# A decoder trunk in float32 by split products: some low parts made by an accumulating transfer, and the order of TensorE fixed in four places

## The chip, the cores and the metric

The kernel runs on one core of one Trainium2 chip. The time is device microseconds of that core for one execution of the program, lower is better. The engines are named as in the profile: PE is TensorE (matmuls), PEld its weight loads, DVE is VectorE, ACT is ScalarE, POOL is GpSimd, SP is SyncE (here it only issues transfers).

## The reference

Two layers over x of shape (1, 512, 1024) in float32, with D_FF = 1408:

```python
def swiglu_ffn(h, w_gu, w_down):
    a, b = jnp.split(h @ w_gu, 2, axis=-1)
    return (jax.nn.silu(a) * b) @ w_down

for i in range(DEPTH):                         # DEPTH = 2
    x = x + 0.5 * swiglu_ffn(rms_norm(x, ffn1_norm[i]), ffn1_w_gu[i], ffn1_w_down[i])
    h = rms_norm(x, mix_norm[i])
    x = x + (mla_gla_mixer(h, ...) if i % 2 == 0 else stick_breaking_mixer(h, ...))
    x = x + 0.5 * swiglu_ffn(rms_norm(x, ffn2_norm[i]), ffn2_w_gu[i], ffn2_w_down[i])
    gate = jax.nn.sigmoid(rms_norm(x, ple_norm[i]) @ ple_w_gate[i])
    x = x + gate * (p[i] @ ple_w_proj[i])
return rms_norm(x, final_norm)
```

Each mixer ends in a product with an output matrix (`ev_w_out`, `od_w_qkv`'s partner `od_w_out`); `ple_w_gate` is the gate of the per-layer embedding.

## The kernel before

x stands transposed in eight tiles of 128 x 512 (features by tokens). Every float32 product is three fp32r products (`mm3`, L393 to L395): both operands are split into a high part, which is a rounding copy, and a low part, which is the rest, and high by high, low by high and high by low are summed. For a weight this is `w_cut` (L260, L261): ACT casts the loaded tile `wr` into `wh`, and DVE subtracts, `wl = wr - wh`. A tile is 128 x 1024 (or 768). Eight matmul steps of three are 24 matmuls on one such weight.

Weights go through three stages, in the order of a list `plan` of all of them: SP loads `wr` from memory (L256, at most 8 tiles), `w_split` cuts it at most WS = 4 weights ahead of the product that uses it, and PE uses it. The kinds that matter here are `gu` (first feed-forward's gate and up weights, pairs A and B, ten tiles, of which the first two are cut in quarters at the start), `sg` (units of the other gate and up columns), `pg` (gate of the embedding, eight tiles, layer 0), `oo` (output matrix of layer 1's mixer, eight tiles, of which the first OPEN = 3 are held in other buffers) and `dn`.

`start` and `gates` compute the first 640 columns of layer 0's first feed-forward. `gated` (L790 to L794) then applies the gate to each pair. All other gate and up columns go through `ffn7`, which computes a 2 x 2 block product with seven products instead of eight: B11, B21, T1, T2, B22, T3, T4, in this order in the program. Each uses two units of weights; T1 to T4 need differences of the loaded tiles, which DVE makes in place (`w_term`, L289), before the cut. The other operands are tiles of the normed x: `nvh`, `nvl` for B11 (even tiles of x), `noh`, `nol` for B21 (odd tiles), `nuh`, `nul` for T1 and T2 (both). `Norm7.steps` (L529 to L569) makes them on ACT and DVE as each tile of x gets its last addition, and adds up squares in `sqa` (L489). One product on one group of columns is 2 tiles x 4 steps x 3 matmuls (L704 to L706). After T1, `norm.sums()` sums `sqa` over features with eight small matmuls into `pss` (L587); DVE (L600) and POOL (L602) make the factor `rc` of them, which `close` uses later. B21's result is added by DVE at L724, and copies of the accumulators are made by ACT (L719).

The text of the kernel is not the order that the engines run. The framework's list scheduler places the instructions by its own estimates; where an instruction is made with `tc.keep_in_program_order`, it keeps its place among the others so made. In the kernel before, a small class `Queue` does this for DVE in `ple` only (profile rows of that stretch carry line 123), and `w_pin` for the cuts of T1's weights in the first group of columns. PE's order is the scheduler's.

## Time and profile before

| what | value |
|---|---|
| median of 3 runs | 1315.92 us (1312.94 to 1319.41) |
| profiled execution, its own time | 1318.16 us |
| its span in the trace | 1316.4 us |
| mean granted clock of PE | 0.983 |
| PE busy | 1280.7 us, 97% |
| DVE busy | 910.8 us, 69% |
| ACT busy | 665.1 us, 51% |
| POOL busy | 116.9 us, 9% |
| read from memory | 115.50 MB |

The profiled execution is 2.24 us above the median; 1.8 us of its time lie outside its span. A busy PE is one with a matmul in flight: one on 512 columns follows the last after about 0.23 us at full clock, and one on 384 columns after about 0.17 us.

### The profile page before, as it was taken

The numbers are of one execution on the slowest core, as the hardware profiler recorded it, in microseconds if no ns is written. First come the engines' busy times: TensorE is split into PE (matmuls) and PEld (weight loads), VectorE is DVE, ScalarE is ACT, GpSimd is POOL, SyncE is SP. The second block draws the span as 40 slices with busy tenths as digits, with TensorE's granted clock in tenths as the row PEclk, the third lists the DMA queues.
The fourth block names the chain that finished last, engine by engine and source line by source line (L and its number), as shares of the span: only waits on it lengthen the run. The fifth ranks groups of instructions, "written<-read, shape, count | busy, mean of one in ns | idle before, by whom it ended". The sixth has DMA issues, their size and how long they took to land.

```text
span 1316.4 us, 16266 instructions
## 1 busy us (share of the span) xinstructions
PE 1280.7 (97%) x6212; PEld 1092.2 (83%) x6212; DVE 910.8 (69%) x1316; ACT 665.1 (51%) x1064; POOL 116.9 (9%) x132
## 2 busy tenths in 40 slices
PE   9969999998999999999989999999999999999997
PEld 7869888886888888988868898888888887898886
DVE  6688763579775998654799875445767598885544
ACT  6455352432654565542655553334778556554442
POOL 0001000425350000000000000000111000000000
PEclk9979999999899999999989999999999999999999
DMA  7023343111300032533203343322113003224401
GB/s 290 34 88 117 109 147 106 45 64 41 121 17 17 0 128 97 160 128 111 81 1 128 97 129 111 128 97 96 65 59 102 16 16 128 93 85 142 145 1 64
DMA packets 39454, 118.66 MB, mean 90 GB/s; under 512 B 4615, under 2 KB 5768, under 8 KB 39376
## 3 DMA queue, kind: packets, MB, share of 16 engines
q1 hardware_dynamic: 38016, 114.64, 26.2%
q0 software_dynamic: 640, 1.89, 0.5%
q8 instruction: 49, 0.80, 0.2%
q10 hardware_dynamic: 720, 1.09, 0.2%
q14 instruction: 29, 0.24, 0.1%
HBM read 115.50 MB, written 2.10 MB: 89 GB/s over the span
## 4 chain that ended last, share of the span: by engine, by line
PE 87%; DVE 9%; ACT 2%; issue 1%; SPq 0%; DMA 0%; POOL 0%; POOLq 0%; DVEq 0%; ACTq 0%
PE dn L395 6%; PE dn L394 6%; PE dn L393 6%; PE al L704 5%; PE al L705 5%; PE al L706 5%; PE ga L705 3%; PE ga L704 3%; PE ga L706 3%; PE sqk L393 2%; PE sqk L395 2%; PE sqk L394 2%; PE val L1016 2%; PE val L1018 2%; PE val L1017 2%; DVE wl L261 1%
## 5 line engine op out<-in xcount | busy, mean ns | idle before, releaser
L260 ACT CAST wh<-wr 128x1024 fp32r<-128x1024 f32 (+3 forms) x299 | 275.4, 925 | 362.2 <-PE dn L394 81.5
L261 DVE TENSOR_TENSOR wl<-wr,wh 128x1024 fp32r<-128x1024 f32 (+3 forms) x292 | 312.7, 1075 | 168.1 <-ACT wh L260 167.4
L395 PE MATMUL dn<-gh,wl 128*128 128x512 f32 x352 | 137.4, 390 | 0.3 <-DVE wl L261 0.2
L393 PE MATMUL dn<-gh,wh 128*128 128x512 f32 x352 | 137.0, 392 | 0.7 <-ACT wh L260 0.7
L394 PE MATMUL dn<-gl,wh 128*128 128x512 f32 x352 | 137.2, 390 | 0.0
L289 DVE TENSOR_TENSOR wr<-wr,wr 128x1024 f32<-128x1024 f32 (+1 forms) x88 | 94.9, 1097 | 0.2
L395 PEld LDWEIGHTS dn<-gh,wl 128*128 128x128 f32 x352 | 66.1, 188 | 14.9 <-DVE wl L261 1.2
L393 PEld LDWEIGHTS dn<-gh,wh 128*128 128x128 f32 x352 | 66.0, 188 | 14.5 <-ACT wh L260 1.1
L394 PEld LDWEIGHTS dn<-gl,wh 128*128 128x128 f32 x352 | 66.1, 188 | 13.8 <-DVE gl L401 0.6
L602 POOL TENSOR_TENSOR rc<-v,half 128x4 f32<-128x4 f32 x8 | 11.8, 1480 | 683.5 <-DVE v L600 683.5
L704 PE MATMUL al<-wh,nvh 128*128 128x512 f32 (+1 forms) x176 | 64.6, 367 | 4.7 <-ACT nvh L534 4.7
L705 PE MATMUL al<-wl,nvh 128*128 128x512 f32 (+1 forms) x176 | 64.5, 366 | 0.0
L706 PE MATMUL al<-wh,nvl 128*128 128x512 f32 (+1 forms) x176 | 64.3, 367 | 0.0
L637 DVE SCALAR_TENSOR_TENSOR x<-dn,x 128x512 f32<-128x512 f32 x32 | 22.1, 691 | 40.9 <-PE dn L395 40.9
L393 PE MATMUL sqk<-xnh,wh 128*128 128x512 f32 x128 | 50.2, 393 | 0.0
L395 PE MATMUL sqk<-xnh,wl 128*128 128x512 f32 x128 | 50.0, 390 | 0.0
L394 PE MATMUL sqk<-xnl,wh 128*128 128x512 f32 x128 | 49.9, 390 | 0.0
L704 PE MATMUL ga<-wh,nuh 128*128 128x512 f32 (+1 forms) x88 | 34.6, 406 | 6.3 <-ACT wh L260 6.3
L704 PEld LDWEIGHTS al<-wh,nvh 128*128 128x128 f32 x176 | 33.2, 189 | 8.9 <-ACT nvh L534 5.1
L481 ACT ACTIVATE sq<-x 128x512 f32<-128x512 f32 x64 | 39.2, 622 | 0.0
L1016 PE MATMUL val<-wh,xnh 128*128 128x512 f32 x96 | 37.5, 391 | 0.0
L1018 PE MATMUL val<-wh,xnl 128*128 128x512 f32 x96 | 37.4, 389 | 0.0
(462 smaller groups left out, 3293.6 us busy)
## 6 DMA issues: line engine op xcount, KB each, us to landing
wr<-in_sg SPq DMA_DIRECT2D x48, 512.0 KB, 4.0
wr<-in_sg SPq DMA_DIRECT2D x40, 384.0 KB, 3.3
wr<-in_dn SPq DMA_DIRECT2D x32, 384.0 KB, 3.1
wr<-in_dn SPq DMA_DIRECT2D x32, 320.0 KB, 3.5
wr<-in_od_qk SPq DMA_DIRECT2D x16, 512.0 KB, 3.2
wr<-in_ev_in SPq DMA_DIRECT2D x12, 512.0 KB, 3.5
wr<-in_gu SPq DMA_DIRECT2D x8, 512.0 KB, 7.2
wr<-in_ev_out SPq DMA_DIRECT2D x8, 512.0 KB, 3.2
```

What stands on the lines that cost most here:

```text
L260: pin(act.copy(hi[:, cs], t[:, cs]))
L261: pin(dve.tensor_tensor(lo[:, cs], t[:, cs], f32(hi)[:, cs], op=ALU.subtract))
L289: sub = lambda o, x, y: pin(dve.tensor_tensor(o[:, :n], x[:, :n], y[:, :n], op=ALU.subtract))
L393: pe.matmul(acc, wh, xh, start=start, stop=False, **k)
L394: pe.matmul(acc, wh, xl, start=False, stop=False, **k)
L395: pe.matmul(acc, wl, xh, start=False, stop=stop, **k)
L481: ins = act.activation(sq, x[m], AF.Square)
L704: pe.matmul(o, h[:, cs], wh[:, ws], start=begin, stop=False, skip_group_check=True)
L705: pe.matmul(o, h[:, cs], wl[:, ws], start=False, stop=False, skip_group_check=True)
L706: pe.matmul(o, lw[:, cs], wh[:, ws], start=False, stop=end, skip_group_check=True)
L1016: pe.matmul(accs[b], xn[k][0][:, bs], wh[:, ws], start=k == 0, stop=False)
L1018: pe.matmul(accs[b], xn[k][1][:, bs], wh[:, ws], start=False, stop=k == KD - 1)
```

## The change

Two things.

First, for three kinds of weight (`gu` from the third tile on, `pg`, and the five `oo` tiles that are not held) the low part is made another way. ACT casts `wh` as before, then ACT writes `wl = -wh`, and POOL issues a transfer that adds the weight from memory to `wl` (512 KB, the same bytes that SP has loaded). 8 + 8 + 5 = 21 subtractions of DVE become 21 ACT instructions and 21 transfers. The others, `sg` and `dn` among them, stay.

Second, PE gets the same `Queue`, and for the first group of columns of each of the four `ffn7` its matmuls of B11, B21, T1 and T2 keep the order of the program. `norm.sums()` moves behind T2. (In layer 0's first feed-forward `rc` is there already, so there it is not called.)

```diff
+        def __init__(self, engine):
+            self.engine, self.kept = engine, False
         def __getattr__(self, name):
-            call = getattr(nc.vector, name)
+            call = getattr(self.engine, name)
...
-    dve = Queue()
+    dve, pe = Queue(nc.vector), Queue(nc.tensor)
...
+    def w_cut_dma(t, src, n, hi, lo):
+        act.copy(hi[:, :n], t[:, :n])
+        act.activation(lo[:, :n], f32(hi)[:, :n], AF.Copy, scale=-1.0)
+        pool.dma_start(lo[:, :n], src, accum_op=ALU.add)
...
             ready[i] = parts
+        elif plan[i][0] in BY_DMA and needs[i] > FIRST:
+            ready[i] = w_tiles()
+            w_cut_dma(t, loads[needs[i] - 1][0], n, *ready[i])
         else:
...
         for gi, (_, n) in enumerate(groups):
             two = lambda name: [bank(name) for _ in range(2)]
+            pe.kept = gi == 0
             al = two("al")
             product(al, gi, "B11", True, False)
...
             product(ga, gi, "T1", True, False)
+            c22 = copies(ga, n)
+            product(al, gi, "T2", False, False)
             if rc is None:
                 rc = norm.sums()
-            c22 = copies(ga, n)
-            product(al, gi, "T2", False, False)
+            pe.kept = False
             c12 = copies(al, n)
...
+BY_DMA = ("pg", "oo", "gu")
```

Three places show what this does to the order of instructions.

ACT at the start of the program, where the casts of the third to the sixth `gu` tile stand (`wr` is the loaded tile, `wh` its high part, `sq` a square for the norm). Before:

```order
L260 CAST wh_236<-wr_226 128x1024
L260 CAST wh_242<-wr_228 128x1024
L260 CAST wh_248<-wr_230 128x1024
L260 CAST wh_260<-wr_232 128x1024
L481 ACTIVATE sq_266<-x_72 128x512
```
With the change:

```order
L280 CAST wh_236<-wr_226 128x1024
L281 ACTIVATE wl_237<-wh_236 128x1024
L280 CAST wh_243<-wr_228 128x1024
L281 ACTIVATE wl_244<-wh_243 128x1024
L280 CAST wh_250<-wr_230 128x1024
L280 CAST wh_263<-wr_232 128x1024
L281 ACTIVATE wl_251<-wh_250 128x1024
L281 ACTIVATE wl_264<-wh_263 128x1024
```
The negations stand between the casts and in front of the squares. On PE, the first products with these weights (A and B are the accumulators, `xnh` and `xnl` the parts of x) are now in this order, and the first with a low part comes after the high ones of three tiles; before it came third:

```order
L404 MATMUL A_300<-xnh_127,wh_236 128x512
L405 MATMUL A_300<-xnl_129,wh_236 128x512
L404 MATMUL B_332<-xnh_127,wh_243 128x512
L405 MATMUL B_332<-xnl_129,wh_243 128x512
L404 MATMUL A_364<-xnh_127,wh_250 128x512
L405 MATMUL A_364<-xnl_129,wh_250 128x512
L406 MATMUL A_300<-xnh_127,wl_237 128x512
L404 MATMUL A_300<-xnh_141,wh_236 128x512
L405 MATMUL A_300<-xnl_143,wh_236 128x512
```
DVE in the first feed-forward, first group (`nul`, `nwl`, `nvl`, `nu` are operands of the norm's steps; `wr<-wr,wr` a difference of weights). Before:

```order
L560 SCALAR_TENSOR_TENSOR nw_546<-x_75,gains,nu_567 128x256
L567 TENSOR_TENSOR nul_574<-nu_567,nuh_571 128x512
L261 TENSOR_TENSOR wl_694<-wr_254,wh_693 128x768
L569 TENSOR_TENSOR nwl_548<-nw_546,nwh_547 128x256
L532 TENSOR_TENSOR nv_577<-nv_577,ne_578 128x256
L289 TENSOR_TENSOR wr_256<-wr_356,wr_256 128x768
L538 TENSOR_TENSOR nvl_584<-nv_577,nvh_582 128x512
L558 SCALAR_TENSOR_TENSOR nu_586<-x_77,gains,ne_578 128x256
L289 TENSOR_TENSOR wr_254<-wr_396,wr_254 128x768
L559 TENSOR_TENSOR nu_586<-nu_586,nv_577 128x256
L289 TENSOR_TENSOR wr_356<-wr_470,wr_356 128x768
```
With the change:

```order
L571 SCALAR_TENSOR_TENSOR nw_554<-x_75,gains,nu_575 128x256
L578 TENSOR_TENSOR nul_582<-nu_575,nuh_579 128x512
L580 TENSOR_TENSOR nwl_556<-nw_554,nwh_555 128x256
L543 TENSOR_TENSOR nv_585<-nv_585,ne_586 128x256
L549 TENSOR_TENSOR nvl_592<-nv_585,nvh_590 128x512
L569 SCALAR_TENSOR_TENSOR nu_594<-x_77,gains,ne_586 128x256
L570 TENSOR_TENSOR nu_594<-nu_594,nv_585 128x256
L571 SCALAR_TENSOR_TENSOR nw_595<-x_77,gains,nu_594 128x256
L578 TENSOR_TENSOR nul_604<-nu_594,nuh_601 128x512
```
The three differences and the low part of the first piece, and a fourth difference right behind it (`wr_258`), have left this run of the norm's steps; they now stand behind its end.

PE in layer 1's second feed-forward, first group (`be` is B21's accumulator, `ga` T1's). Before:

```order
L705 MATMUL be_9460<-wl_9423,noh_9351 128x512
L706 MATMUL be_9460<-wh_9422,nol_9352 128x512
L704 MATMUL ga_9497<-wh_9427,nuh_9263 128x512
L705 MATMUL ga_9497<-wl_9428,nuh_9263 128x512
L706 MATMUL ga_9497<-wh_9427,nul_9268 128x512
L704 MATMUL ga_9497<-wh_9427,nuh_9311 128x512
L704 MATMUL be_9459<-wh_9422,noh_9402 128x512
L705 MATMUL be_9459<-wl_9423,noh_9402 128x512
L704 MATMUL be_9460<-wh_9422,noh_9402 128x512
L705 MATMUL be_9460<-wl_9423,noh_9402 128x512
```
With the change:

```order
L124 MATMUL be_9480<-wh_9443,noh_9372 128x512
L124 MATMUL be_9480<-wl_9444,noh_9372 128x512
L124 MATMUL be_9480<-wh_9443,nol_9373 128x512
L124 MATMUL be_9480<-wh_9443,noh_9423 128x512
L124 MATMUL be_9480<-wl_9444,noh_9423 128x512
L124 MATMUL be_9480<-wh_9443,nol_9424 128x512
L124 MATMUL be_9481<-wh_9393,noh_9273 128x512
L124 MATMUL be_9481<-wl_9394,noh_9273 128x512
```
Before, B21's last step (`noh_9402`, from the last tile of x) comes behind both tiles' other steps and four matmuls of T1; with the change it comes fourth in B21's first tile, ahead of the whole second tile and of all of T1.

## Rows read from the trace of the kernel before

**Rows 1.** The page: busy time, share, instructions; then the chain.
```profile
PE 1280.7 (97%) x6212; PEld 1092.2 (83%) x6212; DVE 910.8 (69%) x1316; ACT 665.1 (51%) x1064; POOL 116.9 (9%) x132
...
PE 87%; DVE 9%; ACT 2%; issue 1%; SPq 0%; DMA 0%; POOL 0%; POOLq 0%; DVEq 0%; ACTq 0%
```

**Rows 2.** PE's waits: what for, us in total, times, longest.
```profile
PE ga L704 <- ACT wh L260: 6.3, 2, 5.1
PE al L704 <- ACT nvh L534: 4.7, 1, 4.7
```

**Rows 3.** Windows: engines busy (us), clock, DMA share, GB/s.
```profile
453.00:480.00 27.00, 27.00 (x123) 22.24 (x123) 24.41 (x28) 17.10 (x20) 1.92 (x1) 1.00 0.43 156
...
900.00:1040.00 140.00, 140.00 (x721) 120.98 (x720) 93.59 (x144) 102.34 (x199) 17.65 (x32) 1.00 0.21 72
...
1073.00:1095.00 22.00, 18.73 (x79) 14.66 (x78) 21.93 (x33) 12.58 (x19) 1.93 (x1) 0.93 0.00 0
```

**Rows 4.** Timeline, start of the program, second weight pair (start, us, engine).
```profile
15.20 1.05 ACT L260 CAST wh<-wr 128x1024 fp32r<-128x1024 f32 x1 [0.42 <-DMA wr<-in_gu]
...
18.35 0.39 PE L393 MATMUL A<-xnh,wh 128*128 128x512 f32 x1
...
18.81 0.39 PE L395 MATMUL A<-xnh,wl 128*128 128x512 f32 x1
```

**Rows 5.** DMA issues, us to landing: 12 to 24 us; whole span; timeline of POOL.
```profile
wr<-in_gu SPq DMA_DIRECT2D x6, 512.0 KB, 7.9
...
craw<-in_consts POOLq DMA_DIRECT2D x3, 256.0 KB, 3.1
...
82.66 0.54 POOL L376 DMA_DIRECT2D craw<-in_consts  x1 [0.59 <-DVE bb L793]
```

**Rows 6.** Timeline, first feed-forward, DVE, then the wait of PE.
```profile
69.12 0.95 DVE L261 TENSOR_TENSOR wl<-wr,wh 128x768 fp32r<-128x768 f32 x1
...
70.66 0.95 DVE L289 TENSOR_TENSOR wr<-wr,wr 128x768 f32<-128x768 f32 x1
...
75.00 0.95 DVE L289 TENSOR_TENSOR wr<-wr,wr 128x768 f32<-128x768 f32 x1
...
81.08 0.68 DVE L790 TENSOR_TENSOR a<-A,R 128x512 f32<-128x512 f32 x1
...
85.36 1.01 PE L704 MATMUL ga<-wh,nuh 128*128 128x384 f32 x2 [5.06 <-ACT wh L260]
```

**Rows 7.** Timeline, around layer 1's first feed-forward: DVE, then PE.
```profile
654.57 1.23 DVE L123 TENSOR_TENSOR wl<-wr,wh 128x1024 fp32r<-128x1024 f32 x1 [0.57 <-ACT wh L260]
...
679.68 0.75 DVE L123 SCALAR_TENSOR_TENSOR nol<-x,gains,noh 128x512 fp32r<-128x512 f32 x1
...
685.28 1.28 DVE L724 TENSOR_TENSOR r<-be,r 128x512 f32<-128x512 f32 x2
...
671.19 0.39 PE L704 MATMUL be<-wh,noh 128*128 128x512 f32 x1
...
676.71 0.73 PE L704 MATMUL ga<-wh,nuh 128*128 128x512 f32 x2 [1.28 <-ACT wh L260]
...
685.42 1.75 PE L587 MATMUL pss<-ones,sqa 128*128 128x2 f32 x8 [1.98 <-DVE sqa L123]
...
697.93 0.39 PE L706 MATMUL al<-wh,nul 128*128 128x512 f32 x1
```

**Rows 8.** Timeline, layer 1's second feed-forward: DVE, then PE.
```profile
1084.80 0.75 DVE L556 SCALAR_TENSOR_TENSOR nol<-x,gains,noh 128x512 fp32r<-128x512 f32 x1
...
1090.39 1.29 DVE L724 TENSOR_TENSOR r<-be,r 128x512 f32<-128x512 f32 x2
...
1078.88 0.39 PE L704 MATMUL be<-wh,noh 128*128 128x512 f32 x1
...
1090.54 0.61 PE L587 MATMUL pss<-ones,sqa 128*128 128x2 f32 x4 [3.27 <-DVE sqa L489]
...
1101.74 0.39 PE L706 MATMUL al<-wh,nul 128*128 128x512 f32 x1
```

More of the change, by code (lines that the diff above doesn't have):

```diff
@@ L110, in tile_kernel @@
     nc = tc.nc
-    act, dve, pe, pool = nc.scalar, nc.vector, nc.tensor, nc.gpsimd
+    act, pool = nc.scalar, nc.gpsimd
     class Queue:
-        kept = False
+        def __init__(self, engine):
+            self.engine, self.kept = engine, False
         def __getattr__(self, name):
-            call = getattr(nc.vector, name)
+            call = getattr(self.engine, name)
             if not self.kept:
```

## The prediction

> **What bounds the kernel now.** I read the page first: PE has a matmul in flight for 97% of the span, and 87% of the chain that ends last is PE's [rows 1]. So work taken off DVE (69% busy) is worth something only where PE waits for DVE, and a wait added to PE costs its full length. Then PE's waits, for these places: the two largest in the products of `ffn7` are 6.3 us for a cast of weights and 4.7 us for `nvh` [rows 2]. Then the timeline where the change touches the program: the start, for whose `gu` weights the list has no wait at all [rows 4], and the first groups of columns, where 1.98 and 3.27 us of waiting for the squares come to those two [rows 6 to 8]. All of these waits, 16 us, stand in the first groups that the change reorders.
>
> A second cost goes with each longer wait. From 1073 to 1095 us, where the 3.27 us wait is the only one to speak of, the granted clock is 0.93 in the mean, so PE is at the lower of its two levels for part of it: 0.07 x 22 = 1.5 us lost [rows 3]. I count 1.5 us for each such spell.
>
> **The change, part by part.**
>
> *Opening, +5.1.* Before, ACT casts the third `gu` tile at 15.20 in 1.05 us, DVE makes its low part, and PE starts on this weight at 18.35 and on its low part at 18.81 without a wait [rows 4]. With the change ACT casts to 16.25, negates to 17.30 (there is no such negation in the trace; it reads and writes 128 x 1024 as the cast does, so I take the cast's 1.05), and POOL issues in 0.54 us [rows 5], at 17.84. PE can in the meantime do six high products, which at 0.227 us (two from 18.35 to 18.81) [rows 4] would end at 19.71; the last two need the cast of the fifth tile, the fifth ACT instruction of 1.05 from 15.20, 20.45, and are done by 20.9. Then it needs the sum in `wl`. How long an accumulating transfer takes, no row shows. The nearest from below: 256 KB on POOL's queue landed after 3.1 us. The nearest from above: 512 KB issued by SP in this same stretch landed after 7.9 us, with its queue full [rows 5]. I take 5.5, the middle: POOL's queue has nothing ahead of it, but the loads of SP are running. It lands at 23.3, 3.6 us later than the 19.71 that PE would have reached; with one slow spell 5.1. Ends: 20.94, which costs 1.2, and 25.74, which costs 6.0 and two spells, 9.0. Below nothing it can't be, since cast, negation and issue alone end behind 17.84 and the landing is behind 20.9 at either end. The second transfer is issued after the negation that ends at 19.40 and lands at 25.4, and B's low part is asked for 22 products after 23.3, at 28.3: hidden, as all later ones, which have three weights of 24 products, some 16 us, ahead of them. If a transfer took over 14 us, this cover would be gone.
>
> On the price of the transfer the Trainium skill speaks against my middle: its page "DMA: Bandwidth & Descriptors", section "Anatomy of one DMA — SWDGE (gpsimd) path", gives about 2.0 us and bytes by 436 GB/s, an estimate of 3.2 us for 512 KB, which would make the opening 1.3 and the sum 7.8. The same page, section "Issuing engines are not separate DMA queues", says that all transfers interleave on the same 16 DMA engines whoever issues them; the 7.9 us of the loads in this stretch agree with that, and I follow the rows.
>
> *First feed-forward, layer 0, -2.* Five DVE instructions leave the run of the norm's steps: the low part at 69.12 and four differences, 70.66 to 75.00, 0.95 us each, together 4.75 [rows 6]. DVE is what PE waits for there, so the first wait (4.7 us) nearly goes. But they come back: `a` starts at 76.3 instead of 81.08, and from it to the second unit of T1, which PE waited for until 85.36, there are now three more of them, 2.85 us. PE goes on at 85.36 - 4.75 + 2.85 = 83.5, 1.9 earlier. Ends: -4.75 if none comes back in PE's way, +1 if the strict order of B21 costs what it can't fill.
>
> *Second feed-forward, layer 0, +1.* PE is full for 27 of 27 us, DVE for 24.41 [rows 3]: there is no wait to win, and the strict order takes away products that PE used to slip in. Ends 0 and 2.0 (as the wait at 685.42 [rows 7]).
>
> *Embedding's gate, 0.* DVE loses eight subtractions, but at 654.57, behind the last of them, it sits idle 0.57 us until ACT's cast [rows 7]: it had caught up, so what runs behind starts as before. Eight negations are ACT's, whose chain gets at most one, 1.05, longer; it is the upper end.
>
> *First feed-forward, layer 1, +3.* B11 ends and B21 begins at 671.19 [rows 7]. In the strict order nine products of 0.227 follow, to 673.2; the next step needs `nol` of the last tile, which DVE has ready at 680.43 [rows 7]. PE used to do steps of T1 in this time; now it waits 7 us. The 13 products behind it end B21 at 683.4, T1's first unit ends at 684.8 (six more), and its second unit needs a low part that now stands on DVE behind the additions, which end at 686.56 [rows 7], and a difference and itself, 1.2 each as at 654.57: 689.0. From there 42 products end T2 at 698.5; a spell of low clock more, 1.5, and the eight `pss` matmuls, now behind T2 (1.05 as at 1090.54 [rows 8]), make 701.0. Before, T2 ended at 697.93 + 0.23 = 698.2 with `pss` done [rows 7]. That is 2.8; I take 3. Ends 0, if the waits hide in each other, and 5.
>
> *Layer 1's mixer, +1.5.* Five negations, 5.25 us, go onto ACT, which is busy 102.34 of 140 us while PE is full [rows 3]. Some will stand in the softmax-like chain of a head. Ends 0 and 5.25. DVE's relief there is worth nothing: nothing waits for it.
>
> *Second feed-forward, layer 1, +3.* The same by its rows: B21 begins at 1078.88; nine products later, at 1080.9, PE waits for the last tile's `nol`, ready at 1085.55: 4.6 us. B21 ends at 1088.5, T1's first unit at 1089.9; the additions end at 1091.68, the low part is there at 1094.1, T2's end 42 products later at 1103.6, with `pss` 1104.7. Before: 1101.74 + 0.23 = 1102.0, two products of B22 in it, so 1101.5 [rows 8]. I take the difference, 3.2, as 3, since the 3.27 us wait and its spell give way to waits of 4.6 and 4.2. Ends +1 and +5.
>
> *Memory.* 21 transfers of 512 KB are 11 MB beside the 115.50 MB that are read now in 1316 us: hidden outside the opening.
>
> Sum: 5.1 - 2 + 1 + 0 + 3 + 1.5 + 3 = 11.6, on the profiled execution's 1318.16: 1329.8. That one is 2.24 above the median of the runs, so 1327.5, **1328** in round numbers, against 1315.92.
>
> **The rivals.**
>
> *Quiet transfers (chance 0.18).* The first transfer lands in the 3.1 us of POOL's own row, and the mixer hides its negations: 1.2 instead of 5.1, 0 instead of 1.5, the sum is 6.2, 1322. For it: POOL's queue is empty. Against: the full queue of loads in those microseconds. The Trainium skill's formula above ("DMA: Bandwidth & Descriptors", same section) is on this side too.
>
> *Slow adding transfers (0.15).* A transfer that reads both sides takes twice the longest row, 15.8 us: the first low part comes at 33.6, 13.9 late, with three spells 18.4; the sum becomes 24.9, 1341. Then also the later ones exceed their cover of 14 us a little. For it: no row of an adding transfer exists. Against: nothing but the plain transfers.
>
> *DVE sets the pace and the change frees it (0.12), faster.* If DVE is late for the whole length of the gate and the mixer's end, the 8 and 5 subtractions of 1.2 that leave pull the norm's last step forward. It decides at the tenth product of B21: if `nol` is there at 673.2 instead of 680.43 and at 1080.9 instead of 1085.55, the strict order costs nothing, the waits of 3.27, 1.98 and 1.28 go with two spells, 9.5, the first feed-forward gives 4.75, and only the opening's 5.1 is against it: -9.2, 1307 [rows 6 to 8]. For it: what PE waits for in these groups comes, through a cast or not, from DVE. Against: the 0.57 us idle at 654.57, and that nothing between it and 680.43 is removed.
>
> The remaining 0.05 is that waits and gains come out even. The forecast itself has 0.50.
>
> **How the numbers follow.** What a measurement of this kernel can tell from no change is about 0.5%, 6.6 us. Slower by more: nearly all of the forecast (0.47), the slow transfers (0.15) and a third of the quiet ones (0.06): 0.68. Within: the rest of the quiet ones, the even case, the edge of the forecast: 0.20. Faster: the last rival: 0.12. The range goes from 1312 (just under 1313.4, the opening quiet and every other term at its lower end) to 1341 (slow transfers); outside lie the fast case and half of the slow one, about 2 in 10.
>
> **What would show it.** In the profile of the changed kernel: a new wait of PE at about 20 us for POOL's transfer, 2 to 6 us, and the clock lower behind it; the waits for `pss` gone; new waits in B21 for `noh` or `nol` of the last tile, near 675 to 690 and 1085 to 1100; DVE busy some 24 us less, ACT some 22 more. It would be wrong if the first low part landed before 21 us, if B21's fourth step came without a wait in both places, or if ACT's share in the mixer put PE to wait by more than 5 us.

## The result and the profile after

The changed kernel takes 1329.49 us in the median of four runs (1329.28 to 1330.70), against 1315.16 us of four runs before (1312.94 to 1319.41): a ratio of 1.0107, 95% interval 1.0089 to 1.0125. It is slower by 14 us. The profiled execution took 1329.65 us with a span of 1327.8; its own difference to the profiled execution before is 11.5 us, and the traces account for that one.

The page of the changed kernel, engines and chain, where [rows 1] stood before:

```profile
PE 1280.6 (96%) x6212; PEld 1088.9 (82%) x6212; DVE 887.6 (67%) x1295; ACT 685.5 (52%) x1085; POOL 130.3 (10%) x153
...
PE 81%; DVE 12%; ACT 3%; issue 2%; DMA 1%; POOL 0%; SPq 0%; POOLq 0%; DVEq 0%; ACTq 0%
```

DVE lost 23 us and ACT got 20 more, as the 21 subtractions and negations should make it. PE is busy as long as before, and its share of the chain fell from 87% to 81%: it waits more. The list of its waits (what for, us in total, times, longest), to be held against [rows 2]:

```profile
PE al L124 <- ACT nvh L545: 8.1, 3, 4.4
...
PE A L406 <- DMA wl<-in_gu: 5.6, 1, 5.6
...
PE be L124 <- ACT noh L557: 5.1, 2, 3.5
...
PE ga L124 <- DVE wl L262: 3.9, 3, 1.5
...
PE be L124 <- DVE nol L567: 2.2, 1, 2.2
...
PE be L124 <- DVE nol L124: 1.9, 1, 1.9
```

A wait of 5.6 us for the first transfer is new, and so are those in B21 (`be`) for `noh` and `nol`; the waits for `pss` and the 6.3 us for a cast are gone. The wait for `nvh` has grown from 4.7 to 8.1 us.

To see where the time goes I cut both traces at the same matmuls: the first on the third `gu` tile, B11 of the first and second groups of the feed-forwards, the first of each mixer and of its output product. What lies between the stretches shown takes the same time to 0.1 us in both, and what lies ahead of the first to 0.2. The columns are start and end, length, busy time of PE, PEld, DVE, ACT and POOL (instructions), PE's granted clock, share and rate of the DMA. Before:

```profile
18.35:63.33 44.98, 44.98 (x203) 37.31 (x202) 30.56 (x46) 20.96 (x34) 1.04 (x1) 1.00 0.31 116
63.33:107.37 44.04, 34.13 (x170) 32.08 (x169) 37.53 (x57) 22.70 (x38) 8.13 (x11) 0.84 0.33 102
201.02:393.04 192.02, 182.80 (x993) 156.63 (x992) 133.26 (x241) 83.22 (x149) 71.49 (x67) 0.96 0.20 65
438.59:477.73 39.14, 39.14 (x178) 32.35 (x176) 36.55 (x44) 22.80 (x29) 1.92 (x1) 1.00 0.30 108
665.75:714.25 48.50, 44.78 (x177) 35.65 (x176) 43.84 (x55) 26.95 (x36) 1.92 (x1) 0.89 0.26 87
858.12:1036.11 177.99, 177.99 (x884) 151.95 (x884) 109.70 (x163) 114.69 (x213) 19.58 (x33) 1.00 0.24 80
1073.44:1117.83 44.39, 41.12 (x177) 33.08 (x176) 41.03 (x52) 25.82 (x35) 1.93 (x1) 0.96 0.28 95
```

And with the change:

```profile
18.17:72.55 54.38, 47.38 (x203) 38.22 (x202) 23.04 (x40) 28.83 (x42) 8.02 (x9) 0.94 0.68 173
72.55:113.98 41.43, 32.86 (x170) 31.05 (x169) 37.13 (x57) 22.78 (x38) 7.01 (x11) 0.88 0.34 109
207.66:396.56 188.90, 181.02 (x993) 154.66 (x992) 134.20 (x241) 83.14 (x149) 71.85 (x67) 0.97 0.20 66
442.11:482.70 40.59, 39.62 (x178) 32.28 (x176) 36.84 (x44) 23.08 (x29) 1.01 (x1) 1.00 0.32 104
670.70:719.74 49.04, 42.18 (x177) 33.87 (x176) 43.78 (x55) 25.91 (x34) 1.04 (x1) 0.93 0.27 86
863.57:1044.36 180.79, 179.47 (x884) 151.59 (x884) 103.77 (x157) 116.96 (x214) 20.19 (x35) 1.00 0.30 91
1081.70:1129.27 47.57, 42.28 (x177) 33.98 (x176) 41.26 (x52) 26.01 (x35) 1.04 (x1) 0.93 0.28 89
```

In this order they are the opening, the first feed-forward's first group, the even mixer, the second feed-forward's first group, the first and, after the odd mixer, the second of layer 1. The differences of their lengths:

| stretch | forecast | measured | PE idle, before and after | lost to the low clock, before and after |
|---|---|---|---|---|
| opening | +5.1 | +9.4 | 0 and 7.0 | 0 and 3.3 |
| first group, layer 0, first | -2 | -2.6 | 9.9 and 8.6 | 7.0 and 5.0 |
| even mixer | 0 | -3.1 | 9.2 and 7.9 | 7.7 and 5.7 |
| first group, layer 0, second | +1 | +1.5 | 0 and 1.0 | 0 and 0 |
| first group, layer 1, first | +3 | +0.5 | 3.7 and 6.9 | 5.3 and 3.4 |
| odd mixer | +1.5 | +2.8 | 0 and 1.3 | 0 and 0 |
| first group, layer 1, second | +3 | +3.2 | 3.3 and 5.3 | 1.8 and 3.3 |

PE idle is length less PE's busy time; the last column is one minus the clock, times the length. It also counts time at the low clock in which PE only waits and loses nothing, so it is an upper bound, and the two columns do not add up to a difference of lengths. The seven differences add up to 11.6. The even mixer is not touched by the change; what happens there is told below.

### The profile page after: what moved, and what is told of

It reads as the page before. It is cut to its first block, busy times and chain, and to the rows that moved or that the text cites. A ratio compares the mean times of both kernels' runs of the same rounds, so it can differ in the third digit from the quotient of the medians.

```text
span 1327.8 us, 16320 instructions
## 1 busy us (share of the span) xinstructions
PE 1280.6 (96%) x6212; PEld 1088.9 (82%) x6212; DVE 887.6 (67%) x1295; ACT 685.5 (52%) x1085; POOL 130.3 (10%) x153
## 4 chain that ended last, share of the span: by engine, by line
PE 81%; DVE 12%; ACT 3%; issue 2%; DMA 1%; POOL 0%; SPq 0%; POOLq 0%; DVEq 0%; ACTq 0%
PE dn L406 6%; PE dn L405 6%; PE dn L404 6%; PE al L717 4%; PE al L716 4%; PE al L715 4%; PE ga L716 2%; PE ga L717 2%; PE ga L715 2%; PE sqk L404 2%; PE sqk L406 2%; PE sqk L405 2%; DVE wl L262 2%; PE al L124 2%; PE val L1029 2%
## 5 line engine op out<-in xcount | busy, mean ns | idle before, releaser
L261 ACT CAST wh<-wr 128x1024 fp32r<-128x1024 f32 (+3 forms) x278 | 253.7, 915 | 326.3 <-PE dn L405 77.1
L262 DVE TENSOR_TENSOR wl<-wr,wh 128x1024 fp32r<-128x1024 f32 (+3 forms) x275 | 291.2, 1063 | 160.0 <-ACT wh L261 159.4
L404 PEld LDWEIGHTS dn<-gh,wh 128*128 128x128 f32 x352 | 66.1, 188 | 14.5 <-ACT wh L261 1.1
L717 PE MATMUL al<-wh,nvl 128*128 128x384 f32 (+1 forms) x144 | 52.1, 362 | 0.0
L715 PE MATMUL al<-wh,nvh 128*128 128x384 f32 (+1 forms) x144 | 52.1, 362 | 0.0
L716 PE MATMUL al<-wl,nvh 128*128 128x384 f32 (+1 forms) x144 | 52.1, 362 | 0.0
L1030 PE MATMUL val<-wl,xnh 128*128 128x512 f32 x96 | 37.4, 390 | 0.0
L280 ACT CAST wh<-wr 128x1024 fp32r<-128x1024 f32 x21 | 21.9, 1046 | 28.1 <-PE A L405 10.4
```

The source lines that it names most:

```text
L261: pin(act.copy(hi[:, cs], t[:, cs]))
L262: pin(dve.tensor_tensor(lo[:, cs], t[:, cs], f32(hi)[:, cs], op=ALU.subtract))
L404: pe.matmul(acc, wh, xh, start=start, stop=False, **k)
L715: pe.matmul(o, h[:, cs], wh[:, ws], start=begin, stop=False, skip_group_check=True)
L716: pe.matmul(o, h[:, cs], wl[:, ws], start=False, stop=False, skip_group_check=True)
L717: pe.matmul(o, lw[:, cs], wh[:, ws], start=False, stop=end, skip_group_check=True)
```

## The experiments

All are built from the changed kernel, with parts put back. Where a stage is spoken of, it is cut at the same matmuls as above.

**The order alone.** No weight by transfer:

```diff
-BY_DMA = ("pg", "oo", "gu")
+BY_DMA = ()
```

> The order of PE is fixed as in the change, and no weight is made by a transfer. Theory (transfers and order cost apart from each other): the opening and the mixer of layer 1 are as before (0 each), the first feed-forward of layer 0 gains 2 to 3 us, the second of layer 0 loses 1.5, those of layer 1 lose 0.5 and 3: about +2 in all, 1317, ratio 1.000 to 1.004. Rival (the order is a gain and only the transfers cost): ratio below 0.998, with the waits in B21 of layer 1 gone once ACT has no negations. Rival (the gain of the first feed-forward came from DVE's lost subtractions): that stage 0 or slower, ratio 1.004 or more.

Measured: 1318.72 us, ratio 1.0033 (1.0021 to 1.0045). The windows of the first groups of layer 0's first feed-forward and layer 1's two:

```profile
63.16:104.59 41.43, 32.85 (x169) 30.89 (x168) 37.23 (x57) 22.78 (x38) 7.29 (x11) 0.88 0.35 109
662.05:712.51 50.46, 43.58 (x178) 34.44 (x177) 43.89 (x55) 27.06 (x36) 1.01 (x1) 0.90 0.26 84
1071.68:1119.37 47.69, 42.38 (x177) 34.05 (x176) 41.26 (x52) 26.03 (x35) 1.02 (x1) 0.93 0.28 88
```

Against before that is -2.6, +2.0 and +3.3. Layer 0's second feed-forward is 1.5 longer, as in the changed kernel; the opening is 44.98 us as before, and the odd mixer 178.01. Only layer 1's first group differs from the changed kernel (+2.0 against +0.5); why is told below, with `pg`. So the first feed-forward's gain belongs to the order, not to DVE's lost subtractions (this kernel has all of them), and so do the losses of the other three groups.

**The transfers alone.** The two `pe.kept` lines are taken out, and `norm.sums()` goes back behind T1:

```diff
-            pe.kept = gi == 0
...
+            if rc is None:
+                rc = norm.sums()
             c22 = copies(ga, n)
             product(al, gi, "T2", False, False)
-            if rc is None:
-                rc = norm.sums()
-            pe.kept = False
```

> All 21 low parts by transfer, PE's order left to the scheduler and the sums where they were. Theory: opening +9, mixer of layer 1 +2.8, the feed-forwards' first groups within 1 of before: +11 to +12, 1327, ratio 1.009. Rival (the order costs most of it): ratio 1.005 or less. Rival (DVE's lost subtractions are worth something once PE may slip in other work): the first groups of the feed-forwards each 1 to 3 faster than before, sum +6 or less.

Measured: 1326.78 us, ratio 1.0090 (1.0075 to 1.0105). Layer 1's first group:

```profile
676.35:722.36 46.01, 41.71 (x177) 32.93 (x176) 43.70 (x55) 25.71 (x34) 1.94 (x1) 0.96 0.27 92
```

The opening is 9.5 longer (54.48 us), and so is the odd mixer by 2.8; the first groups of layer 0's two feed-forwards and of layer 1's second are as before to 0.2. Layer 1's first comes out 2.5 shorter, which was not expected; its idle time is 4.3 against 3.7 before, and the mean clock 0.96 against 0.89. What lies behind it is told below, with `pg`. The two halves of the change add up within their intervals: 0.33% and 0.90% against 1.07% together.

**gu alone, oo alone, pg alone.** `BY_DMA` with one name each, no order.

> Only the eight gu tiles by transfer, no order. Theory: PE waits 5 to 7 us for the first transfer at about 20 us, one or two slow spells, +9 at the end of the opening and still about +9 at the end: 1324, ratio 1.007. Rival (the wait is absorbed by the first feed-forward, where PE waits for DVE anyhow): +9 at the end of the opening, under +4 behind the first feed-forward, ratio 1.003 or less.

Measured: 1326.39 us, ratio 1.0088 (1.0073 to 1.0102). The opening is 9.8 longer and nothing behind it gives that back: at the odd mixer's end the program is still 11.0 late. The eight `gu` tiles alone cost nearly what all 21 transfers do. The rival, that the first feed-forward's waits take it up, falls: that group is 44.14 us against 44.04 before, only later.

> Only the five oo tiles by transfer, no order. Theory (ACT's five negations stand in the chain of a head): the mixer of layer 1 is 2 to 4 us longer, with waits of PE for exponentials of ACT or low clock, ratio 1.002. Rival (ACT's 27% idle takes them; the 2.8 us of the changed kernel came from a shift of the whole program): 0 to 0.5 us, ratio 1.000.

Measured: 1319.42 us, ratio 1.0036 (1.0023 to 1.0048). The odd mixer:

```profile
856.20:1037.00 180.80, 179.43 (x884) 151.59 (x884) 103.85 (x157) 116.94 (x214) 20.24 (x35) 1.00 0.29 91
```

2.8 us longer than before, and again without any low clock. Its cause is taken up below, with the negations alone. The rest of the 4.9 us of the medians I can't place: in the profiled execution the other stages differ by no more than 1.3 us, nearly all of it low clock.

> Only the eight pg tiles by transfer, no order. With all transfers and no order, the first group of layer 1's first feed-forward was 2.5 us shorter than before, with two slow spells of 3.4 us fewer but a longer wait for the squares. Theory (the gain is real: DVE is freed in the gate): that stage 2 to 3 shorter again, ratio 0.998. Rival (it is only where the slow spell fell): that stage within 1 of before, and after taking half of the low-clock time out of it, the same as before within 0.5; ratio 1.000.

Measured: 1314.94 us, ratio 1.0006 (0.9992 to 1.0019): no difference. The gate of the embedding is as long as before to 0.1 us, as forecast. Layer 1's first group, right behind it, is 2.4 shorter again, and that is not chance. In all four kernels with `pg` by transfer DVE ends the last step of the norm there (the last addition to `sqa`) 18.6 us after the group's beginning, in the ten without it, the kernel before among them, 19.6. The trace of the kernel before shows where that microsecond was (ACT, then DVE; the group begins at 665.75):

```profile
665.72 1.06 ACT L260 CAST wh<-wr 128x1024 fp32r<-128x1024 f32 x1 [2.01 <-PE G L394]
...
666.67 0.62 ACT L562 CAST nuh<-nu 128x512 fp32r<-128x512 f32 x1
...
667.33 0.69 DVE L123 TENSOR_TENSOR nul<-nu,nuh 128x512 fp32r<-128x512 f32 x1 [0.93 <-ACT nuh L562]
```

ACT has a cast of weights in front of `nuh`, and DVE waits 0.93 us for `nuh`. In the changed kernel (its group begins at 670.70) ACT makes `nuh` first and the cast later, and DVE has no such wait:

```profile
669.53 0.62 ACT L573 CAST nuh<-nu 128x512 fp32r<-128x512 f32 x1 [0.88 <-DVE nu L124]
...
670.89 1.03 ACT L261 CAST wh<-wr 128x1024 fp32r<-128x1024 f32 x1
```

The other twelve kernels have the one order or the other, and split the same way; the step ahead of it on DVE (`x`) stands at the same place in all, to 0.1 us. So it is the place of one ACT instruction that moved, and not that DVE has less to do. The group is 2.4 to 2.5 shorter in the three kernels that have `pg` by transfer and PE's order free there; in the six others with PE's order free there it is between the same and 0.9 shorter. How much of the 2.4 is this microsecond and how much a shorter time at the low clock is not separated. The medians show no gain: in this profiled execution layer 1's second group is 1.4 longer, with the clock at 0.93 instead of 0.96, and the even mixer 1.6.

**gu by transfer only from the seventh tile on.** No order.

```diff
-        elif plan[i][0] in BY_DMA and needs[i] > FIRST:
+        elif plan[i][0] in BY_DMA and needs[i] > FIRST + 4:
```

> gu by transfer only from the seventh tile on (four of eight), no order. Theory (only the first transfers meet the wait, later ones have three weights of cover): the opening within 0.3 of before, no wait of PE for a transfer, ratio 1.000. Rival (ACT's negations or the transfers lengthen the chain of the gate that the first feed-forward waits for): opening as before, but its first group 1 to 2 longer, ratio 1.001 or more.

Measured: 1315.63 us, ratio 1.0015 (1.0006 to 1.0024). PE waits for no transfer; the opening is 0.6 longer than before instead of 9.4, 0.3 of it idle. So it is the first transfers that cost, as forecast. The other stages of the profiled execution show no loss; the rest of the 2 us of the medians I can't place.

**A plain copy in place of the adding transfer.** As gu alone, but the transfer overwrites the negation; the low parts then hold whole weights.

```diff
-        pool.dma_start(lo[:, :n], src, accum_op=ALU.add)
+        pool.dma_start(lo[:, :n], src.bitcast(F32R) if False else src)
```

The condition is never true, so this is `src`, copied from float32 into fp32r as the adding transfer adds it.

> As the run with gu alone, instruction for instruction, but the transfers copy the weight over the negation instead of adding to it (so the low parts hold whole weights; the time is what is looked at). It tells whether the landing time in the opening is the adding or the company of SP's loads. Theory (mostly the loads in the same 16 DMA engines, some the adding: adding transfers of 512 KB took 5.2 to 5.9 us in quiet stretches, plain ones of SP 3.2): the first lands 5 to 6.5 us after its issue instead of some 8, PE waits 2.5 to 4 us instead of 5.7. Rival (the loads alone): 8 us and 5 to 6 us of wait. Rival (the adding alone): 3 to 4 us and under 1.5 us of wait.

Measured once: 1322.40 us; the opening is 6.8 us longer than before, where gu alone made it 9.8. POOL's issue of the first transfer and the matmul that waits for it (start, length, in brackets the idle time and what ended it), with the adding transfer (gu alone):

```profile
17.73 0.92 POOL L282 DMA_DIRECT2D wl<-in_gu  x1 [3.58 <-ACT wl L281]
...
26.90 0.80 PE L406 MATMUL A<-xnh,wl 128*128 128x512 f32 x1 [5.73 <-DMA wl<-in_gu]
```

and with the plain copy:

```profile
17.69 0.54 POOL L282 DMA_DIRECT2D wl<-in_gu  x1 [3.35 <-ACT wl L281]
...
25.03 0.80 PE L406 MATMUL A<-xnh,wl 128*128 128x512 f32 x1 [3.89 <-DMA wl<-in_gu]
```

Issued at the same time, the copy lets PE go on 1.9 us earlier, 0.4 of it in the issue itself: 0.54 against 0.92 us. The wait goes from 5.73 to 3.89. So the adding is a third of it; two thirds are there for a plain transfer too. From the start of its issue to its landing the plain one took 7.3 us, the adding one 8.8 to 9.1 in the three kernels that have it first; SP's loads of 512 KB take 3.2 us in a quiet stretch and 7 to 8 here.

**The order in one place.** Only in layer 0's first feed-forward, no transfers, the sums where they were.

```diff
-            pe.kept = gi == 0
+            pe.kept = gi == 0 and (w, l) == (1, 0)
```

> PE's order fixed only in the first group of layer 0's first feed-forward, no transfers, the sums where they were. Theory: that group 2.6 shorter, as in the changed kernel and with the order alone, the other three groups as before: ratio 0.998, about 1312. Rival (what the shorter group wins is lost where the next slow spell falls): the group 2.6 shorter, the end within 1 of before.

Measured: 1312.40 us, ratio 0.9988 (0.9979 to 0.9997): a little faster than both kernels. That group:

```profile
63.14:104.80 41.66, 33.09 (x169) 31.33 (x168) 37.24 (x57) 22.78 (x38) 7.02 (x11) 0.88 0.34 108
```

It is 2.4 shorter; with the order in all four places it was 2.6. In the medians 1.2 us is left of it; the interval, 0.4 to 2.8, has room for all of it.

**B21 left free.** No transfers; the full order in layer 0's first feed-forward; in the other three only from T1 to the sums behind T2.

```diff
+            pe.kept = gi == 0 and (w, l) == (1, 0)
             al = two("al")
...
             ga = two("ga")
+            pe.kept = gi == 0
             product(ga, gi, "T1", True, False)
```

> Order fixed fully in layer 0's first feed-forward, and in the other three only from T1 to the sums behind T2; B11 and B21 are left to the scheduler, which then runs the first three steps of both tiles of B21 ahead of their last step. No transfers. Theory (the strict B21 costs the nine products that it can't slip in, 2.0 us each time): layer 1's first feed-forward +0 instead of +1.95 with the order alone, its second +1.3 instead of +3.3, layer 0's second +0 to +1.5; ratio 0.999 to 1.000. Rival (T1 and T2 in strict order, and the low part of T1's second unit behind the additions, cost most): the three groups within 0.5 of the order alone, ratio 1.003.

Measured: 1323.45 us, ratio 1.0076 (1.0064 to 1.0089). This is slower than the order alone, and my theory of B21 falls: layer 1's groups are 3.6 and 5.5 longer than before, where the whole order made them 2.0 and 3.3 longer. The rival, within 0.5 of the order alone, misses the sizes too. PE's waits in the last group show why (it begins at 1073.87):

```profile
1091.77 0.50 PE L124 MATMUL ga<-wh,nuh 128*128 128x512 f32 x1 [3.64 <-ACT wh L261]
...
1094.42 0.80 PE L124 MATMUL ga<-wl,nuh 128*128 128x512 f32 x1 [2.15 <-DVE wl L262]
```

PE gets through B21 earlier, and then waits 3.64 us for the high part and 2.15 for the low part of T1's second unit. It has that low part 20.6 us after the group's beginning; with the order alone it was 21.0. In both, the end of the group hangs on this unit, whose parts are cut behind the last norm step, and what PE does sooner in B21 only lengthens the wait. That the group is longer still comes from the low clock, which falls on other work: the 17 products of T1 from that low part on take 6.6 us here and 4.0 with the order alone. The clock is 0.66 in the mean from 1090 to 1100 us, on T1; with the order alone it was 0.94 in the ten microseconds that answer to these (1088 to 1098), and 0.83 in the 17 before, where PE waits in B21 anyhow.

**T1 by units of weights.** The order alone, but T1 uses its first unit on both tiles before the second.

```diff
-            for t in range(2):
-                for j in range(KD // 2):
-                    (h, lw), c = norm.side(term, j)
+            turns = [(t, j) for t in range(2) for j in range(KD // 2)]
+            if term == "T1" and gi == 0:
+                turns.sort(key=lambda tj: (tj[1] // 2, tj[0], tj[1]))
+            for t, j in turns:
+                    (h, lw), c = norm.side(term, j)
```

> The order alone, no transfers, but in the first groups T1 runs its first unit of weights on both tiles before its second unit. With B21 left free the first groups of layer 1 came out longer, not shorter, so the strict B21 is not what costs; in every order PE comes to wait for the second unit of T1, whose parts are cut behind the norm's steps. Theory (it is this wait; six more products cover 1.4 us of it): layer 1's feed-forwards +0.5 and +1.9 instead of +1.95 and +3.3, layer 0's second +0 to +1.5, the first as with the order alone; ratio 1.000 to 1.001. Rival (the wait moves on to T2, whose units are cut behind it): as the order alone within 0.5, ratio 1.003.

Measured: 1318.92 us, ratio 1.0035 (1.0023 to 1.0047), the same as the order alone. But the first groups are not the same. Against before they are, in the order of the program, -1.0, +1.5, +1.1 and +1.9; with the order alone -2.6, +1.5, +2.0 and +3.3. In the last group:

```profile
1095.18 0.50 PE L124 MATMUL ga<-wl,nuh 128*128 128x512 f32 x1 [0.59 <-DVE wl L262]
```

The wait for the low part of the second unit goes from 1.5 to 0.6 us, and the group, 47.69 us with the order alone, is 1.4 shorter:

```profile
1074.62:1120.92 46.30, 41.92 (x178) 33.27 (x176) 41.18 (x52) 26.02 (x35) 1.02 (x1) 0.96 0.28 91
```

PE has that low part 20.6 us after the group's beginning instead of 21.0, and behind it 35 products of T1 and T2 instead of 41. The clock, 0.96 in the mean against 0.93, can't be the reason: with the order alone it is 0.70 in the 8.8 us ahead of the low part (1083.84 to 1092.67), in which PE comes to wait anyhow, and 1.00 in the 10.2 us behind it. Layer 1's first group is 0.8 shorter, 49.63 against 50.46; there PE now also waits 0.33 us for the low part of T2's second unit. So in layer 1 the theory comes out (+0.5 and +1.9 were expected), and the rival, within 0.5 of the order alone, doesn't. What the theory left out is layer 0's first group, where T1's order changed too:

```profile
62.99:105.99 43.00, 33.88 (x170) 31.55 (x169) 37.33 (x57) 22.88 (x38) 7.13 (x11) 0.84 0.33 105
```

It is 1.6 longer than with the order alone, with the clock at 0.84 instead of 0.88 and two waits, 0.26 and 0.29 us, for casts of weights that the order alone does not have. What layer 1 gains is mostly lost there, and the medians show nothing.

So, by one trace of each kernel, T1's order is worth about 0.8 of the 2.0 us that layer 1's first group loses, and 1.4 of the second's 3.3. The rest is not separated by a run. On the path of the changed kernel's trace stand two more things: the difference of weights that DVE now makes ahead of the low part, 1.1 us, and the eight `pss` matmuls behind T2, 0.8 us.

**The negations of oo without their transfers.** As oo alone, without the `pool.dma_start` line; the low parts hold minus the high part. The scheduler also placed five matmuls of PE and some ACT instructions of this stretch differently from the run with oo.

> As the run with oo alone, but without the five transfers (the low parts hold minus the high part): the five negations stay on ACT. It tells ACT's share of the mixer's 2.8 us from POOL's, where the instruction that makes la stands behind a transfer whose issue waits for ACT. Theory (both, ACT first): the mixer 1 to 2 us longer than before. Rival (POOL's queue alone): 0 to 0.3. Rival (ACT alone): 2.5 to 3.

Measured once: 1315.27 us. The odd mixer:

```profile
854.89:1033.11 178.22, 178.22 (x884) 152.09 (x884) 104.27 (x158) 117.82 (x216) 18.27 (x33) 1.00 0.23 80
```

0.2 us longer than before, against 2.8 with the transfers. So it is not ACT's time; the rival, POOL's queue alone, had 0 to 0.3. In the run with oo, on POOL and then ACT:

```profile
1003.18 0.91 POOL L282 DMA_DIRECT2D wl<-in_od_out  x1 [3.63 <-ACT lah L410]
...
1004.03 1.05 POOL L1533 TENSOR_TENSOR la<-u,la 128x256 f32<-128x256 f32 x1
...
1001.82 1.05 ACT L281 ACTIVATE wl<-wh 128x1024 fp32r<-128x1024 f32 x1
...
1005.11 0.51 ACT L410 CAST lah<-la 128x384 fp32r<-128x384 f32 x1 [1.94 <-POOL la L1533]
```

The transfer stands on POOL ahead of the two instructions that make `la`, and starts there only when ACT has done the negation (at 1001.82, 1.05 us long) and the cast behind it, which the profile names as what ended the wait. ACT's next instruction needs `la` and waits 1.94 us for it; the chain of the head behind it is late by that, and PE with it. ACT's waits in this stretch, in that run (from 990 to 1040 us):

```profile
ACT lah L410 <- POOL la L1533: 3.9, 3, 1.9
```

Neither the kernel before nor the one with negations alone has this wait. Head by head, PE in the run with oo is level with the kernel before to 0.1 us up to 137 us into the mixer, 0.4 late at the head that begins at 153 us (1009.5), right behind this wait, and 2.7 late at the last one, at 174. PE waits for no transfer in this stretch.

**What is left of the change.** The order in layer 0's first feed-forward, and `pg` by transfer.

> What is left of the change when the parts that cost are taken out: the order only in layer 0's first feed-forward, pg by transfer, the sums where they were. Theory (pg's transfers are worth nothing in either direction, the order of that one group 1 to 2.5 us): as the run with the order in the first group alone, ratio 0.998 to 0.9995. Rival (DVE's freed time in the gate adds to it): 0.997 or less. Rival (the transfers of pg cost through POOL's queue as those of oo do): 1.000 or more.

Measured: 1313.13 us, ratio 0.9992 (0.9981 to 1.0003): as with that order alone. The faster version found is that one, with no transfer at all.

## Why the prediction was right, and where it wasn't

The forecast, 1328 in the range of 1312 to 1341, slower by over 0.5%, came within 2 us of the measured time, and its main terms are in the trace with their signs. The difference between the two kernels was forecast as 11.6 us and is 14.3 in the medians. That it came so near is partly luck: the opening was 4.3 too small and layer 1's first group 2.5 too large, and the terms of layer 0's first feed-forward and of the odd mixer came about in another way than told.

*Opening, forecast +5.1, measured +9.4.* The mechanism is the one told: cast, negation, issue, and PE with nothing to do. ACT's cast and negation, POOL's issue, and PE, where [rows 4, 5] stood before:

```profile
15.80 1.05 ACT L280 CAST wh<-wr 128x1024 fp32r<-128x1024 f32 x1 [1.48 <-DMA wr<-in_gu]
...
16.88 1.06 ACT L281 ACTIVATE wl<-wh 128x1024 fp32r<-128x1024 f32 x1
...
18.25 0.90 POOL L282 DMA_DIRECT2D wl<-in_gu  x1 [4.39 <-ACT wl L281]
...
20.95 0.50 PE L404 MATMUL A<-xnh,wh 128*128 128x512 f32 x1 [1.29 <-ACT wh L280]
...
27.25 0.80 PE L406 MATMUL A<-xnh,wl 128*128 128x512 f32 x1 [5.56 <-DMA wl<-in_gu]
```

The negation takes 1.06 us, as taken. PE goes on at 27.25 instead of the 23.3 worked out. Of these 4 us, 1.3 come ahead of the landing: the cast 0.6 later than in the trace before, 0.3 between negation and issue, and an issue of 0.90 us instead of 0.54. The missized step is the landing: I took 5.5 us behind the issue, from the middle between 3.1 and 7.9; it was 8.1, or 9.0 from the issue's start, as the rows count it. That is above the upper end. The spell of low clock was sized right: behind the wait it cost 0.13 x 12.75 = 1.7 us where I counted 1.5; the rest of the 3.3 in the table lies inside the waits:

```profile
27.25:40.00 12.75, 12.75 (x49) 10.43 (x50) 2.73 (x4) 4.65 (x7) 0.85 (x1) 0.87 1.04 262
```

Of the two rules of the Trainium skill's page "DMA: Bandwidth & Descriptors", the estimate of 3.2 us for 512 KB ("Anatomy of one DMA — SWDGE (gpsimd) path") was too low here by far, 9.0 us with the adding and 7.3 without it. The other rule of that page of the Trainium skill, "Issuing engines are not separate DMA queues", agrees with the trace: POOL's queue was empty and the transfer still took as long as SP's loads (9.0 against 8.0 in the median). Where it is quiet, the adding transfers landed in 5.3 and 5.9 us (medians, the rows of the changed kernel, with SP's plain load of the same size for comparison); the eight of `gu` have a median of 7.3:

```profile
wr<-in_od_out SPq DMA_DIRECT2D x8, 512.0 KB, 3.2
...
wl<-in_pg POOLq DMA_DIRECT2D x8, 512.0 KB, 5.9
...
wl<-in_od_out POOLq DMA_DIRECT2D x5, 512.0 KB, 5.3
```

That the later transfers are hidden held: no other wait of PE for a transfer is in the list.

*First feed-forward, layer 0, -2, measured -2.6* (-2.6 with the order alone, too). The size is right, the path is not, so this is luck. The step "the first wait (4.7 us) nearly goes" failed: DVE's run did get shorter (`a` starts 2.9 us earlier after the group's beginning, not 4.75), but PE, with no products of B21 and T1 to slip in, now waits 4.4 and 3.0 us for `nvh`. What goes is the second wait, 5.06 us for T1's second unit: PE comes to it 21.7 us after the group's beginning instead of 17.0 and finds it ready. In all it idles 1.3 us less and has less time at the low clock.

*Second, layer 0, +1: right* (+1.5); PE, which had no wait there, now waits 0.9 us for the low part of T1's second unit. *Embedding's gate, 0: right* for the gate itself.

*First feed-forward, layer 1, +3, measured +0.5.* Two steps were wrong. The first stands with the gate: "it had caught up, so what runs behind starts as before". With `pg` by transfer the last norm step ends 1.0 us earlier, as shown above, and PE has the low part of T1's second unit 22.4 us after the group's beginning, where I worked out 23.3; with the order alone, without `pg`'s transfers, it was 23.8. The second is "a spell of low clock more", 1.5 us behind that low part: the clock is 0.71 from 684.40 to 693.05, ahead of it, and 1.00 from there to the end of `pss` at 703.73. Ahead of it the low clock costs nothing: it stretches B21's last 13 products from 3.0 to 5.4 us, and the wait for the low part is 1.5 instead of the 4.2 that follow from my times (those in B21 are 5.3 instead of 7). T2 and `pss` end 33.0 us after the beginning, where I had 35.3.

*Odd mixer, +1.5, measured +2.8.* The size was inside its bounds, the reason was not: I put it down to ACT's five negations, and the run with these alone shows 0.2. It is what stands behind a waiting transfer on POOL. The part on the change did not name it, though POOL's order would have shown it.

*Second feed-forward, layer 1, +3: right* (+3.2). The waits in B21 are in the trace, at 1090.97 and 1093.86, as is the one for T1's second unit, where [rows 8] had the one for `pss`:

```profile
1090.97 0.50 PE L124 MATMUL be<-wh,noh 128*128 128x512 f32 x1 [1.62 <-ACT noh L557]
...
1093.86 0.80 PE L124 MATMUL be<-wh,nol 128*128 128x512 f32 x1 [2.16 <-DVE nol L567]
...
1102.57 0.50 PE L124 MATMUL ga<-wl,nuh 128*128 128x512 f32 x1 [1.51 <-DVE wl L262]
```

But the reason that I gave most room, that B21's strict order takes PE's cover away, is not what costs: with B21 free the group is longer still. What made the sum come out is its other step, the low part of T1's second unit behind the additions and a difference. Put at the same beginning, it was forecast for 1094.1 and PE has it at 1094.3; T2 was to end at 1103.6 and ends at 1103.7; `pss` was to end at 1104.7 and ends at 1104.6. In between the waits were shorter (3.8 in B21 and 1.5 for the low part, instead of 4.6 and 4.2), since the low clock stretched B21's end; the low part comes last and hides that.

*Even mixer, 0, measured -3.1.* Nothing there was changed, and in the kernels of this study, in which nothing there was changed either, the same stretch came out between 3.3 us shorter and 1.6 longer than in the trace before, mostly with the time at the low clock. So it does not follow the change: behind the same order of layer 0's first feed-forward it came out from 3.3 shorter to as before. Whether it differs from execution to execution or from kernel to kernel is open, since each kernel has one trace. Without it the profiled executions would lie 14.6 apart, near the 14.3 of the medians.

*The rivals.* Quiet transfers: no, 9 us. Slow ones of 15.8: no for the first; the longest of the eight `gu` transfers took 14.5, and its cover held. DVE freed: no; in layer 1's second group the last norm step came no earlier, and in its first 1.0 us earlier, by the order of ACT, where this rival needed 7.

## What to carry to other kernels

Taking work off an engine that is not what the others wait for brought nothing that the medians show, and what replaced it was waited for at the one place where there is no lead: let such a path begin only where some weights of lead exist (with all eight `gu` tiles the opening was 9.8 us longer, with the last four 0.6). A transfer whose issue waits is an instruction like any other on its engine: look for what is queued behind it, not only at what its data costs (2.8 us in the odd mixer, 0.2 without the transfers). And where a wait is forecast, work out the end of the stage through the last thing that comes late; an earlier wait, or low clock ahead of it, may be hidden by it. For the same reason a mean clock of a stage doesn't say what the low clock cost: see on which side of the last wait it fell.

## What the runs showed of the hardware

- An adding transfer of 512 KB keeps POOL for 0.85 to 0.94 us at its issue, a plain one of the same shape for 0.53 to 0.60 us. Where it is quiet it lands 2 to 3 us later than SP's plain one (5.3 and 5.9 against 3.2 in the changed kernel); how much of that is the adding and how much the path through POOL no run shows. Beside SP's loads the first one took 9.0 us, and a plain one through POOL 7.3.
- Time at the lower of PE's two levels follows waits of several microseconds but is not fixed by them: with the same instructions the even mixer had a mean granted clock of 0.96 to 0.98, with lengths from 3.3 us shorter to 1.6 longer than in the trace before, and a stage with longer waits could have less of it (layer 1's first group: 0.89 with 3.7 us idle before, 0.96 with 4.3 us idle with `pg` alone). Differences of two or three microseconds in a stage with waits have to be read with the clock beside them.
